# A hybrid transformer in fp32 on one core: the norm split into three steps among products, modulation rows in buffers of their own, one low part completed by an accumulating DMA, two whole pairs ahead of the blocked ones

## The chip, the cores and the metric

One NeuronCore of a Trainium2 chip runs the whole program in one launch. The metric is device time in microseconds (us), the median of several executions.

## The reference

Two layers work on 256 latent tokens and 256 context tokens of width 1024. Every branch is preceded by an RMS norm whose scale, shift and gate come from a modulation vector (`silu(c) @ mod_w`, nine vectors of 1024 for each layer and stream):

```python
lat = lat + 0.5 * mod[:, 0, 2] * _swiglu(_modulate(lat, norm_g[i, 0], mod[:, 0, 0], mod[:, 0, 1]), w13, w2)
...   # the same for the context tokens cx
h = _modulate(lat, norm_g[i, 1], mod[:, 1, 0], mod[:, 1, 1])
y = _short_conv_mixer(h, ...)                 # layer 0
y, _ = _gqa_mixer(h, hc, False, ...)          # layer 1: keys of both streams, queries of lat
lat = lat + mod[:, 1, 2] * y
lat = lat + 0.5 * mod[:, 2, 2] * _swiglu(_modulate(lat, norm_g[i, 2], ...), w13, w2)

def _swiglu(h, w13, w2):
    gte, up = jnp.split(h @ w13, 2, axis=-1)
    return (jax.nn.silu(gte) * up) @ w2       # hidden width 2816 = 22 x 128
```

In order there are: swiglu (0,0), the convolution mixer, swiglu (0,1), swiglu (1,0), attention, swiglu (1,1). The last one and the last projection are for the latent tokens alone.

## The kernel before

Everything is held with features on the 128 partitions and tokens along the free axis: `x` is 8 tiles of 128 features by 512 tokens. The first 256 columns (s = 0) are the latent tokens, the other 256 (s = 1) the context. The weights are fp32. Each is split into a rounded high part and a low part (`split`: ACT rounds, line 92; DVE subtracts, line 93), and each product is three matmuls, high·high, high·low and low·high (`mm3`, lines 116 to 118).

**Weights.** `load_raw` (line 86) brings 1 MB through SP's DMA queue into one of three buffers `wr`. `load_w` splits them into four halves `wh`/`wl`. The same three `wr` buffers also take the modulation rows.

**Modulation.** Each of the 236 units (`mod_unit`, line 136, tile `junk`) is one DVE instruction over 128 x 1024: a row block times the broadcast `silu(c)`, summed. Four units (two for a vector that one stream alone needs) share a 1 MB load. They are dealt out by `tick(n)`, which stands between products, and `mod_ready` makes those up that a consumer still lacks.

**A swiglu** goes in thirds of 8, 7 and 7 hidden tiles ("pairs": one gate tile and one up tile of `w13`), and after each third `project` multiplies by the matching part of `w2` and adds to `x` (`finish`, line 438). For 512 tokens a pair is either computed as it is (`w13_mm`, tiles `pg` and `pu`, 96 matmuls of 256 columns or 48 of 512) or as a `Pair`: a 2 x 2 blocked product with seven block products instead of eight (tiles `p` and `q`, 84 matmuls of 256 columns). For that DVE makes sums of weight blocks (`ws`, lines 548, 554, 556), and `Blocks.sums` makes sums of activation blocks (T1 to T4) once. The block A22 gets its own `w4h`/`w4l`. `head` uses A11 and A12 with the s = 0 activations, `five` to `four` the sums, and `four` of one pair comes after `six` of the next.

**The joint between two stages.** `tail_norm` is called as the last feature tiles of `x` are finished. `square_add` sums squares; `rms_inv` (line 226) adds them over partitions by four one-column matmuls (`ss`, line 231), takes the root on ACT and the reciprocal on DVE, and spreads the result by four matmul records (line 242). Then the normed activations are made (`t`, line 250, and `bh`/`bl` or `hh`/`hl`). Steps wait in the list `pending`, and `flush` runs them at chosen places. In the last project of a swiglu the last two feature tiles (m = 6, 7) are done for s = 0 first and then for s = 1, so that the norm of s = 0 runs beside the products of s = 1. The norm of s = 1 runs beside the s = 0 products of the next swiglu's pair 0 and the `head`s of pairs 1 and 2.

**Order.** A framework schedules the traced instructions: it keeps dependences, hands out buffers and chooses each engine's order when the program is built. Each engine then runs its own queue in order.

## Time and profile before

| | |
|---|---|
| three timed runs | 1613.83, 1616.15, 1619.61 us (median 1616.15) |
| the profiled execution | 1611.37 us, of which its span is 1609.5 |
| PE (matmuls) busy | 1576.1 us, 98% |
| DVE busy | 1332.4 us, 83% |
| ACT busy | 722.2 us, 45% |
| POOL | 0.2 us, 4 instructions |
| HBM read | 244.77 MB, 153 GB/s |

PE is the matrix engine, PEld its weight loads, DVE the vector engine, ACT the scalar engine, POOL the general one, SP the queue that issues nearly all DMAs. `PEclk` or "granted clock" is the share of full clock that the matrix engine was given. A matmul's recorded duration overlaps the next one's, so its cost is the distance from start to start. A line number in a profile is that of the kernel it was taken from.

### The profile page before, as it was taken

The numbers are of one execution on the slowest core, as the hardware profiler recorded it, in microseconds if no ns is written. First come the engines' busy times: TensorE is split into PE (matmuls) and PEld (weight loads), VectorE is DVE, ScalarE is ACT, GpSimd is POOL, SyncE is SP. The second block draws the span as 40 slices with busy tenths as digits, with TensorE's granted clock in tenths as the row PEclk, the third lists the DMA queues.
The fourth block names the chain that finished last, engine by engine and source line by source line (L and its number), as shares of the span: only waits on it lengthen the run. The fifth ranks groups of instructions, "written<-read, shape, count | busy, mean of one in ns | idle before, by whom it ended". The sixth has DMA issues, their size and how long they took to land.

```text
span 1609.5 us, 25613 instructions
## 1 busy us (share of the span) xinstructions
PE 1576.1 (98%) x10566; PEld 1450.1 (90%) x10566; DVE 1332.4 (83%) x2035; ACT 722.2 (45%) x1110; POOL 0.2 (0%) x4
## 2 busy tenths in 40 slices
PE   9999999999999999999999999999999999899999
PEld 6788998999888889899899889889899897789999
DVE  4988778879998889799797999898898789965554
ACT  5532452544322365335255465245254455454443
POOL 0000000000000000000000000000000000000000
PEclk9999999999999999999999999999999999999999
DMA  8456235234565513353433413452432463755453
GB/s 320 162 183 209 80 122 180 90 135 152 177 221 186 180 41 117 132 183 100 168 120 115 154 54 131 172 195 96 156 129 96 180 214 108 270 201 185 169 194 109
DMA packets 38277, 248.77 MB, mean 155 GB/s; under 512 B 5136, under 2 KB 6928, under 8 KB 12304
## 3 DMA queue, kind: packets, MB, share of 16 engines
q1 hardware_dynamic: 35712, 245.38, 43.7%
q10 hardware_dynamic: 2448, 1.76, 0.4%
q8 instruction: 82, 1.34, 0.3%
q14 instruction: 35, 0.29, 0.1%
HBM read 244.77 MB, written 1.05 MB: 153 GB/s over the span
## 4 chain that ended last, share of the span: by engine, by line
PE 82%; DVE 12%; DMA 3%; ACT 2%; issue 1%; DVEq 0%; ACTq 0%; SPq 0%
PE py L117 7%; PE py L116 7%; PE py L118 7%; PE p L116 6%; PE p L118 6%; PE p L117 6%; PE q L118 5%; PE q L116 5%; PE q L117 5%; DVE junk L136 4%; DVE wl L93 3%; PE pg L117 2%; PE pg L118 2%; PE pg L116 2%; PE pu L117 2%; PE pu L118 2%
## 5 line engine op out<-in xcount | busy, mean ns | idle before, releaser
L92 ACT ACTIVATE wh<-wr 128x1024 fp32r<-128x1024 f32 (+2 forms) x274 | 274.4, 1014 | 395.0 <-PE py L117 108.7
L93 DVE TENSOR_TENSOR wl<-wr,wh 128x1024 fp32r<-128x1024 f32 (+2 forms) x274 | 318.2, 1167 | 97.0 <-ACT wh L92 96.4
L136 DVE CUSTOM_DVE_ANT_0 junk<-wr,scbc,modb 128x1024 bf16<-128x1024 f32 x236 | 302.5, 1282 | 39.6 <-DMA wr<-in_modT 37.0
L117 PE MATMUL py<-gl,wh 128*128 128x512 f32 (+1 forms) x746 | 263.2, 353 | 0.0
L116 PE MATMUL py<-gh,wh 128*128 128x512 f32 (+1 forms) x746 | 263.1, 353 | 0.0
L118 PE MATMUL py<-gh,wl 128*128 128x512 f32 (+1 forms) x746 | 262.9, 352 | 0.0
L93 DVE TENSOR_TENSOR wl<-ws,wh 128x1024 fp32r<-128x1024 f32 x112 | 136.8, 1223 | 27.3 <-ACT wh L92 27.0
L118 PEld LDWEIGHTS py<-gh,wl 128*128 128x128 f32 x746 | 141.1, 189 | 19.1
L116 PEld LDWEIGHTS py<-gh,wh 128*128 128x128 f32 x746 | 141.2, 189 | 18.6
L117 PEld LDWEIGHTS py<-gl,wh 128*128 128x128 f32 x746 | 141.2, 189 | 18.0
L92 ACT ACTIVATE wh<-ws 128x1024 fp32r<-128x1024 f32 x112 | 117.8, 1057 | 76.4 <-PE p L117 34.2
L116 PE MATMUL p<-th,wh 128*128 128x256 f32 x448 | 126.8, 283 | 0.0
L117 PE MATMUL p<-tl,wh 128*128 128x256 f32 x448 | 126.8, 283 | 0.0
L118 PE MATMUL p<-th,wl 128*128 128x256 f32 x448 | 126.6, 283 | 0.0
L117 PE MATMUL q<-bl,wh 128*128 128x256 f32 x336 | 95.2, 283 | 0.0
L116 PE MATMUL q<-bh,wh 128*128 128x256 f32 x336 | 95.1, 283 | 0.0
L118 PE MATMUL q<-bh,wl 128*128 128x256 f32 x336 | 95.1, 283 | 0.0
L438 DVE SCALAR_TENSOR_TENSOR x<-py,G,x 128x256 f32<-128x256 f32 x168 | 74.2, 480 | 21.4 <-PE py L118 21.2
L116 PEld LDWEIGHTS p<-th,wh 128*128 128x128 f32 x448 | 86.0, 192 | 0.5 <-ACT sg L584 0.2
L117 PEld LDWEIGHTS p<-tl,wh 128*128 128x128 f32 x448 | 86.0, 192 | 0.3
L118 PEld LDWEIGHTS p<-th,wl 128*128 128x128 f32 x448 | 85.9, 192 | 0.0
L116 PE MATMUL pg<-hh,wh 128*128 128x256 f32 (+1 forms) x240 | 75.8, 316 | 4.6 <-ACT hh L260 4.6
(236 smaller groups left out, 4001.3 us busy)
## 6 DMA issues: line engine op xcount, KB each, us to landing
wr<-in_w SPq DMA_DIRECT2D x88, 1024.0 KB, 4.9
wr<-in_modT SPq DMA_DIRECT2D x67, 1024.0 KB, 4.9
wr<-in_w2b SPq DMA_DIRECT2D x32, 896.0 KB, 4.6
wr<-in_w2a SPq DMA_DIRECT2D x16, 1024.0 KB, 4.9
wr<-in_cw_cx SPq DMA_DIRECT2D x8, 1024.0 KB, 4.9
wr<-in_mod SPq DMA_DIRECT2D x5, 1024.0 KB, 7.4
wr<-in_cw_b SPq DMA_DIRECT2D x4, 1024.0 KB, 4.8
wr<-in_cw_out SPq DMA_DIRECT2D x4, 1024.0 KB, 4.9
```

The source lines that it names most:

```text
L92: nc.scalar.activation(out=hi, in_=src, func=AF.Copy)
L93: nc.vector.tensor_tensor(out=lo, in0=src, in1=hi.bitcast(F32), op=ALU.subtract)
L116: nc.tensor.matmul(ps, wh, mh, start=first, stop=False, **kw)
L117: nc.tensor.matmul(ps, wh, ml, start=False, stop=False, **kw)
L118: nc.tensor.matmul(ps, wl, mh, start=False, stop=last, **kw)
L136: nc.vector.tensor_tensor_reduce(out=junk, in0=raw[:, j * D : j * D + D], in1=scbc[:, v, :], scale=1.0, scalar=modb[:, l, col : col + 1], ...
L438: nc.vector.scalar_tensor_tensor(out=x[:, m, s * S : s * S + S], in0=ps[:, o : o + S], scalar=g[:, m, s : s + 1], in1=x[:, m, s * S : s * ...
```

## The change

1. `rms_inv` becomes `rms_sum` and `rms_all`. The norm of each stream now stands in `pending` as three steps (sums; spread and first half; second half), and `flush(1)` calls one at a time among products. The first matmul behind a step, and the norm's own matmuls, are held in program order.
2. The last project before a norm does its last three feature tiles (m = 5, 6, 7) by streams instead of its last two (`late` 3).
3. In swiglus (0,1) and (1,0) pairs 0 and 1 are computed as they are, ahead of the blocked ones, where only pair 0 was; the activation sums T1 to T4 and the weight sums are made in pieces between their products.
4. The low part of A22: ACT writes minus the high part, and a DMA issued by POOL adds the weights to it from HBM. DVE's subtraction (128 x 512) goes.
5. Modulation rows come by 512 KB into two buffers `mr` of their own; `wr` has two buffers instead of three. The first modulation vectors, which the matrix engine makes, are loaded by halves into the pool of activation tiles.
6. The calls of `tick` move within attention (none is left in the loop over heads), and the last projection's `ev` is 0.6 instead of 1.

```diff
-        raw = wp.tile([P, 2048], F32, name=nm("wr"), tag="wr", bufs=3)
+        raw = wp.tile([P, 2048], F32, name=nm("wr"), tag="wr", bufs=2)
...
+    pin = [False]
     def mm3(ps, w, m, first, last, more=False):
...
-        nc.tensor.matmul(ps, wh, mh, start=first, stop=False, **kw)
+        i = nc.tensor.matmul(ps, wh, mh, start=first, stop=False, **kw)
+        if pin[0]:
+            tc.keep_in_program_order(i)
+            pin[0] = False
...
+    def load_mod(l, ch, kt):
+        raw = mp.tile([P, D], F32, name=nm("mr"), tag="mr", bufs=2)
+        o = kt % 2 * D
+        nc.sync.dma_start(raw, a["modT"][l, ch * 4 + kt // 2, :, o : o + D])
+        return raw
...
-    def rms_inv(s, parts):
+    def held(ins):
+        return tc.keep_in_program_order(ins)
+    def rms_sum(s):
         pq = psmall("ss")
+        parts = accs[s], accs[s, "last"]
...
+        return pq, ri
+    def rms_all(pq, ri):
         for i in range(2):
-            nc.tensor.matmul(
+            held(nc.tensor.matmul(
...
     class Blocks:
-        def sums(self):
+        def sums(self, n):
...
-            tt(out=b11, in0=b12, in1=b11, op=ALU.subtract)
-            keep("T1", b11)
...
+            if n == 0:
+                tt(out=b11, in0=b12, in1=b11, op=ALU.subtract)
+                keep("T1", b11)
+            elif n == 1:
...
-    def flush(n=9):
+    def flush(n=99):
         while pending and n:
             pending.pop(0)()
+            pin[0] = True
             n -= 1
...
+                keep = []
+                def spread():
+                    keep.append(rms_all(*keep.pop()))
+                    rest(0, keep[0])
+                if s:
                     flush()
-                    pending.append(both_parts)
+                pending.extend(
+                    (lambda: keep.append(rms_sum(s)), spread, lambda: rest(1, keep[0]))
+                )
+                if (l, j) == (1, 2):
+                    flush()
...
-            wl = [get(m) for m in (6, 7)]
+            ms = range(KT - late, KT)
+            wl = [get(m) for m in ms]
...
             for s in range(2):
-                for i in range(2):
+                for i, m in enumerate(ms):
                     ps = psum("py")
-                    products(ps, wl[i], range(nk // 2), s * S, s * S + S)
-                    flush(1)
-                    products(ps, wl[i], range(nk // 2, nk), s * S, s * S + S)
-                    finish(6 + i, ps, s * S, s * S + S, gate, tail)
+                    products(ps, wl[i], range(cut), s * S, s * S + S)
+                    if i:
+                        flush(1)
+                    products(ps, wl[i], range(cut, nk), s * S, s * S + S)
+                    if i == 0:
+                        flush(1)
+                    finish(m, ps, s * S, s * S + S, gate, tail)
...
     class Pair:
...
-            split(*self.w["A22"], a22)
+            nc.scalar.activation(out=hi, in_=a22, func=AF.Copy)
+            nc.scalar.activation(out=lo, in_=hi.bitcast(F32), func=AF.Copy, scale=-1.0)
+            nc.gpsimd.dma_start(out=lo, in_=self.src[:, T2:1024], accum_op=ALU.add)
...
     def ffn(l, b, h, tot, gate, tail, gs=(), ev=1.5):
...
-                    w = load_w(a["w13"][l, b, 0])
-                    gs = [new_pair("g")]
-                    pp = psum("pg"), psum("pu")
-                    w13_mm(pp, w, h, range(KT), 0, S)
+                    w = [load_w(a["w13"][l, b, 0])]
+                    gs = [new_pair("g") for _ in range(2)]
+                    pp = [(psum("pg"), psum("pu")) for _ in range(2)]
+                    w13_mm(pp[0], w[0], h, range(4), 0, S)
+                    flush(1)
+                    w13_mm(pp[0], w[0], h, range(4, 6), 0, S)
+                    flush(1)
+                    w13_mm(pp[0], w[0], h, range(6, KT), 0, S)
+                    w.append(load_w(a["w13"][l, b, 1]))
+                    w13_mm(pp[1], w[1], h, range(KT), 0, S)
                     flush()
-                    for i in (1, 2):
-                        heads.append(Pair(a["w13"][l, b, i], h))
-                        heads[-1].head()
-                    w13_mm(pp, w, h, range(KT), S, T2)
-                    w13_post(pp, gs[0], 0, T2)
+                    h.sums(0)
+                    w13_mm(pp[0], w[0], h, range(KT), S, T2)
+                    w13_post(pp[0], gs[0], 0, T2)
+                    heads.append(Pair(a["w13"][l, b, 2], h))
+                    h.sums(1)
+                    heads[0].sums(0)
+                    w13_mm(pp[1], w[1], h, range(KT), S, T2)
+                    w13_post(pp[1], gs[1], 0, T2)
+                    heads[0].head()
+                    h.sums(2)
+                    heads[0].sums(1)
...
     def mod_pe(ch, q):
-        raw = load_raw(a["mod0"][ch, q])
+        raw = []
+        for i in range(2):
+            raw.append(hot("pm", F32))
+            nc.sync.dma_start(raw[i], a["mod0"][ch, q, :, i * 1024 : i * 1024 + 1024])
...
-                if n == 11:
-                    flush()
+                if n in (5, 11, 17):
+                    flush(1)
...
         if hd:
             mix(hd - 1, pts.pop(hd - 1))
-        tick(2)
...
-        by_pairs("wo"), lambda k, c0, c1: aos[k], KT, lazy_gate(1, 1), tail_norm(1, 2, hn), S, 0, 1,
+        by_pairs("wo"), lambda k, c0, c1: aos[k], KT, lazy_gate(1, 1), tail_norm(1, 2, hn), S, 0, 0.6,
```

## The prediction

> **What bounds the kernel now.** First the page's totals and its slices:
>
> ```profile
> span 1609.5 us, 25613 instructions
> PE 1576.1 (98%) x10566; PEld 1450.1 (90%) x10566; DVE 1332.4 (83%) x2035; ACT 722.2 (45%) x1110; POOL 0.2 (0%) x4
> ...
> DVE  4988778879998889799797999898898789965554
> ```
>
> PE is the bound, with DVE close behind it in many slices. PE's price per matmul comes from two full stretches of the view by windows (length, then busy time and count of PE, PEld, DVE, ACT, POOL; granted clock; DMA share and GB/s):
>
> ```profile
> 480.00:520.00 40.00, 40.00 (x178) 33.13 (x177) 34.25 (x52) 11.52 (x13) 0.00 (x0) 1.00 0.55 187
> ...
> 1440.00:1480.00 40.00, 40.00 (x336) 40.00 (x335) 23.63 (x31) 18.05 (x26) 0.00 (x0) 1.00 0.57 194
> ```
>
> 512 columns cost 40/178 = 0.2247 us, 256 columns 40/336 = 0.119. Next, the stretches where PE loses time. I count what is lost as length minus PE busy, plus (1 - clock) times length:
>
> ```profile
> 565.00:605.00 40.00, 36.46 (x276) 35.25 (x276) 34.13 (x50) 27.65 (x48) 0.00 (x0) 0.91 0.16 53
> 915.00:962.00 47.00, 42.64 (x317) 40.89 (x316) 42.89 (x64) 32.06 (x56) 0.00 (x0) 0.93 0.21 69
> 1055.00:1070.00 15.00, 13.42 (x88) 11.95 (x87) 14.96 (x21) 6.07 (x9) 0.00 (x0) 1.00 0.47 163
> ...
> 1333.00:1376.00 43.00, 35.18 (x224) 29.78 (x223) 43.00 (x108) 24.88 (x57) 0.00 (x0) 0.94 0.34 121
> 1376.00:1405.00 29.00, 26.88 (x210) 25.90 (x209) 26.84 (x46) 13.47 (x21) 0.00 (x0) 0.97 0.76 273
> 1405.00:1420.00 15.00, 10.28 (x62) 9.42 (x61) 14.91 (x30) 8.40 (x16) 0.00 (x0) 0.77 0.68 249
> ```
>
> Lost: 3.5 + 3.6 = 7.1 (joint into swiglu (0,1)); 4.4 + 3.3 = 7.7 (joint into (1,0)); 1.6; 7.8 + 2.6 = 10.4 (loop over heads); 2.1 + 0.9 = 3.0 (projection); 4.7 + 3.5 = 8.2 (joint into (1,1)). Together 38.0 us, nearly all that is to be had behind the start. The heads' 43.00 us are DVE's own bound. The same windows for the tile junk alone show modulation's share there (DVE busy, clock, DMA):
>
> ```profile
> 1333.00:1376.00 43.00, 12.48 (x10) 0.94 0.34 121
> ```
>
> PE's timeline names what ended the waits (start, length, instruction, idle time before it):
>
> ```profile
> 578.30 0.60 PE L242 MATMUL ss<-ident,ri 128*128 128x128 f32 x4
> 583.25 0.58 PE L116 MATMUL pg<-bh,wh 128*128 128x256 f32 x1 [3.03 <-ACT bh L92]
> ...
> 929.11 0.38 PE L231 MATMUL ss<-ones,sq 128*128 128x1 f32 x2 [1.22 <-ACT sq L214]
> ```
>
> From the spread of the context's norm to its first block lie 4.95 us, 5.65 plus to its low part (584.55). Last, DVE's distances from start to start, in its timeline: 1024 elements 1.14 us, 512 elements 0.60, a unit 1.20.
>
> ```profile
> 1059.33 1.22 DVE L93 TENSOR_TENSOR wl<-wr,wh 128x1024 fp32r<-128x1024 f32 x1
> 1060.47 0.87 DVE L438 SCALAR_TENSOR_TENSOR x<-py,G,x 128x256 f32<-128x256 f32 x2
> 1061.25 0.68 DVE L554 TENSOR_TENSOR ws<-wr,ws 128x512 f32<-128x512 f32 x1
> 1061.85 0.69 DVE L93 TENSOR_TENSOR w4l<-wr,w4h 128x512 fp32r<-128x512 f32 x1
> 1062.45 0.69 DVE L556 TENSOR_TENSOR ws<-wr,ws 128x512 f32<-128x512 f32 x1
> 1063.06 1.28 DVE L136 CUSTOM_DVE_ANT_0 junk<-wr,scbc,modb 128x1024 bf16<-128x1024 f32 x1
> 1064.26 0.09 DVE L136 DVE_READ_ACCUMULATOR2_ANT mod<- 128x1 f32 x1
> ```
>
> **PE's added work.** A whole pair is 96 matmuls of 256 columns, a blocked one 84: two pairs more as they are cost 24 x 0.119 = 2.9 us. `late` 3 splits one more feature tile in four projections: 3 x 21 + 24 = 87 matmuls of 512 become pairs of 256, 87 x (0.238 - 0.2247) = 1.2. PE is full there, so all of it counts: **+4.0**.
>
> **The joints into (0,1) and (1,0).** I read the built order of both kernels on each engine. Before, 11 products (1.3 us) stand between the context's spread and the first product that needs it. After, 54 do (6.5 us), against the 4.95 to 5.65 us above. DVE's queue between the reciprocal and the first block's low part now holds one weight split, one or two weight sums, seven `t`, one block sum and that low part: 1.14 + 0.60 + 7 x 0.40 + 1.14 + 1.14, and a unit in (0,1) alone, 1.20 = 8.0, beginning some 1 us ahead of the spread. The remaining stall lies between 0 and 1.5 us. The four sums matmuls no longer follow the last square directly, which ends the 1.22 above. I leave 2 us, clock included, in each joint: **-5.1 and -5.7**. Of the clock: in 915:962 no wait of PE exceeds 1.22 us, and 0.93 was granted all the same, so small stalls are charged for clock too.
>
> The Trainium skill, "TensorE: Matmul & The Clock Gate" (What's actually happening), has the clock halved after an idle window of about 3.4 us. By that rule stalls under it would cost no clock and each joint would give about 1 us more; 915:962 speaks against it.
>
> **Modulation moved ahead.** With buffers of their own the rows are no longer held behind weights. In DVE's built order all 236 units stand ahead of the last third of (0,1); before, 23 of them lay in 1333:1420. All their instructions move with them: 134 half loads on SP where 67 were, 0.33 us of issue each on SP, which waits mostly for buffers. Taken out of the late stages: at 1055 the 1.6 us go, **-1.6**. In the heads DVE's 43.0 less 12.5 is 30.5 us, below PE's own 43 - 10.4 = 32.6; I leave 3 us for the softmax chain, **-7.4**. In the projection 0.5 stays: **-2.5**. At the joint into (1,1) nothing covers the norm's chain, before or after; three units go ahead of it, and I leave 5 us: **-3.2**.
>
> What moves in must fit. From the first `seven` to the first residual update, the second third of (0,0) had 7 units among 55.0 us of DVE (counts by the distances above) and now has 21 among 70.7, for 66.2 us of PE. The last third has 70.5 likewise, and (0,1)'s first third 65.4 for 62.0. The surplus is 4.5 + 4.3 + 3.4 = 12.2 us. Behind the first of these the projection needs 35.1 of 42.5 us of DVE, and weights are split 3 to 5 us ahead, so most is absorbed: between 0 and 12.2, I take **+3**, nearer to 0 because 440:480 ran with DVE 39.61 of 40 busy and PE full.
>
> **A22's low part.** DVE loses 54 x 0.60 = 32 us, already in the sums above. ACT gains 54 x 0.63 = 34 us on 722, covered by its idle half. POOL waits for ACT's copy; only other such DMAs queue behind it, and PE's `four` waits for it two pairs (20 us) after its buffer comes free. The nearest landings are 3.8 us (rt, 64 KB) and 4.9 (1 MB): hidden, 0. If it took over 14 us, `four` would wait for the rest. **Two `wr` buffers:** a load holds one for 4.9 + 1.06 (ACT) + 2 x 1.14 = 8.2 us, so two feed a weight every 4.1 us, and (1,1), the fastest, uses one in 48 x 0.119 = 5.7: 0. SP's new waits on `mr` hold weight loads queued behind them; that is a rival below. **The start:** DMA is 89% busy in the first 40 us. Free loads can gain 4.4 us at most, rows ahead of weights lose as much: 0.
>
> Sum: 4.0 - 5.1 - 5.7 - 1.6 - 7.4 - 2.5 - 3.2 + 3 = -18.5. The profiled execution took 1611.37 us (its span and 1.9 around it), so 1592.9; the median of the runs is 4.8 above it, so **1598** as a median.
>
> **Rivals.**
> *DVE takes it back.* The whole surplus of 12.2 stays and the joints give half: -18.5 + 9.2 + 5.4 = -3.9, 1612. For it: DVE full in the pairs with 0 to 1 us of reserve. Against: 440:480.
> *Rows wait (slower).* DVE meets a unit whose row has not landed. The waits list has this:
>
> ```profile
> DVE junk L136 <- DMA wr<-in_modT: 37.0, 21, 4.8
> ```
>
> That is 1.76 us a time. In the thirds named and (0,1)'s second (16 units), 76 units now stand on 38 loads; a wait there delays splits, `four` and SP's next weight, with no reserve. Eleven such waits eat the gain; half of the 38 give -18.5 + 33.4, so 1631. Against: the units stand apart there, and a row has several us to land.
> *POOL holds DVE up (slower).* The trace has no POOL work. If each accumulating DMA held DVE by one 512-element instruction (0.69 us) in the 34 pairs of (0,0) and (0,1), that is 23.5: +5.0, 1621. From 0.54 us it decides.
>
> The Trainium skill, "SBUF — State Buffer" (Who interferes with whom), says that DVE and POOL lock each other out of a shared port for whole instructions, and that DMAs issued by POOL wait for their descriptors; no run here shows it yet.
>
> **How the numbers follow.** 0.3% (4.8 us) is about what a measurement can tell. My forecast has 0.68, its own range 1580 to 1609 (the low end: all 38.0 back and no surplus). DVE taking it back has 0.14: 0.06 faster, 0.07 same, 0.01 slower. Rows waiting 0.10, slower. POOL 0.08: 0.02 same, 0.06 slower. Faster 0.74, same 0.09, slower 0.17. With most of the second case inside, the range ends at 1616.
>
> **What would show it.** Windows around both joints should lose about 2 us each with a clock near 1, and no `junk` should stand in the heads, where PE is then the fuller engine. In 160:360 DVE should be over 95% busy with PE still full. PE idle there, released by `wl` behind `junk`, or `mr` loads leading DVE's waits, would prove me wrong; so would `w4l` products waiting for a DMA.

## The result: slower by 0.3%, and the profile after

| | before | after |
|---|---|---|
| median (16 runs each, timed together) | 1614.65 us | 1620.57 us |
| range | 1612.21 to 1619.61 | 1613.48 to 1625.37 |
| profiled execution | 1611.37 (span 1609.5) | 1624.71 (span 1622.9) |

The ratio is 1.0032, 95% interval 1.0019 to 1.0045: slower by 5 to 6 us. The forecast was 1598, with 1616 as the upper end.

The profiled execution of before lies 3.3 us under its median, that of after 4.1 over it. Of the 13.3 us between these two only 5.9 lie between the medians, so a difference of a few us in a single stage below may be of the execution and not of the kernel.

The page of the changed kernel has two lines that answer to those of before:

```profile
span 1622.9 us, 26150 instructions
...
DVE  4899999999899999989888579568577578755554
```

DVE is full for the first half and light afterwards, as forecast, since the units now stand there (the last at 850). The view by windows shows the same stretches as before, moved by what had been lost ahead of them (the columns are those of the prediction). The first two rows are those the prediction had no loss for, the start and the joint into the convolution:

```profile
0.00:40.00 40.00, 33.99 (x176) 22.62 (x177) 16.06 (x44) 20.41 (x37) 0.20 (x4) 0.87 0.80 300
390.00:425.00 35.00, 31.97 (x216) 30.45 (x215) 29.79 (x65) 15.21 (x30) 0.00 (x0) 0.85 0.39 136
577.00:617.00 40.00, 37.34 (x283) 36.76 (x282) 36.74 (x62) 23.65 (x43) 1.74 (x2) 0.91 0.41 121
937.00:984.00 47.00, 44.77 (x360) 44.39 (x359) 37.13 (x57) 31.37 (x54) 1.73 (x2) 0.96 0.33 98
1079.00:1094.00 15.00, 15.00 (x104) 13.95 (x103) 10.06 (x13) 5.43 (x8) 0.00 (x0) 1.00 0.22 71
1350.00:1391.00 41.00, 37.31 (x257) 32.66 (x256) 37.89 (x93) 27.90 (x60) 0.00 (x0) 1.00 0.24 83
1391.00:1418.00 27.00, 27.00 (x225) 26.75 (x226) 17.82 (x33) 14.06 (x25) 0.00 (x0) 1.00 0.23 79
1418.00:1434.00 16.00, 12.76 (x86) 12.30 (x85) 11.13 (x24) 8.20 (x16) 0.00 (x0) 0.79 0.38 132
...
280.00:320.00 40.00, 38.52 (x291) 36.99 (x291) 40.00 (x56) 20.68 (x32) 2.54 (x3) 1.00 0.61 177
```

and before:

```profile
0.00:40.00 40.00, 37.25 (x210) 24.41 (x211) 17.69 (x51) 21.61 (x45) 0.20 (x4) 1.00 0.89 320
380.00:420.00 40.00, 39.79 (x287) 37.28 (x287) 38.65 (x75) 17.70 (x34) 0.00 (x0) 1.00 0.39 135
```

The joint into (1,0) (the 937 row), the rest of (1,0) (1079), the heads (1350), the projection (1391) and the joint into (1,1) (1418) gained. The joint into (0,1) (577) hardly did, the start and the joint into the convolution (390) lost, and inside a pair stretch (280) PE now waits while DVE is busy 40.00 of 40.

To compare kernels stage by stage I take from each trace, for every two matmuls in a row, their distance from start to start less the full-speed distance (0.227 us for 512 columns, 0.120 for 256, 0.110 for one). The sum is what PE lost to waits and clock together, in us. A stage runs from one first `py` to the next, with its joint in it. Each column is one execution.

| PE lost in | before | after | steps only | DMA and `pm` out, start free |
|---|---|---|---|---|
| start, to the first `py` | 22.0 | 29.1 | 24.7 | 25.0 |
| other thirds of (0,0), (0,1) | 0.1 | 9.5 | 2.5 | 2.7 |
| end of (0,0), convolution | 1.9 | 9.7 | 4.7 | 3.2 |
| joint into (0,1), its first third | 7.8 | 9.6 | 3.0 | 6.6 |
| joint into (1,0), its first third | 9.8 | 4.6 | 2.8 | 4.8 |
| rest of (1,0) | 2.9 | 0.2 | 8.7 | 0.2 |
| attention | 15.5 | 11.6 | 26.5 | 13.2 |
| its projection, joint into (1,1) | 11.7 | 6.1 | 7.9 | 6.2 |
| sum | 71.7 | 80.4 | 80.8 | 61.9 |
| span less the sum | 1537.8 | 1542.5 | 1542.3 | 1542.3 |

The last row is PE's own work: 4.7 us more, where +4.0 was forecast. The third and fourth kernels are experiments (e9, which also has item 6 of the change, and e12), told below.

DVE's and PE's waits lists name what is new:

```profile
DVE junk L146 <- DMA mr<-in_modT: 35.9, 26, 2.8
...
PE ss L243 <- ACT sq L222: 6.3, 5, 1.7
PE q L118 <- ACT gm L602: 4.9, 4, 1.6
```

The second leads PE's list. Before, the same wait, of the norm's sums for a square, was

```profile
PE ss L231 <- ACT sq L214: 1.7, 2, 1.2
```

The DMA view of the changed kernel:

```profile
q1 hardware_dynamic: 46080, 245.39, 44.8%
q0 software_dynamic: 7776, 14.16, 5.3%
...
mr<-in_modT SPq DMA_DIRECT2D x134, 512.0 KB, 4.1
...
w4l<-in_w POOLq DMA_DIRECT2D x54, 256.0 KB, 5.1
```

Queue q0 carries the 54 accumulating DMAs. Per MB they held the 16 engines for 0.053 x 1622.9 / 14.16 = 6.1 us, the other loads (q1) for 0.448 x 1622.9 / 245.39 = 3.0 us.

### The profile page after: what moved, and what is told of

Read it like the earlier page. It is cut to its first block, busy times and chain, and to the rows that moved or that the text cites. A ratio compares the mean times of both kernels' runs of the same rounds, so it can differ in the third digit from the quotient of the medians.

```text
span 1622.9 us, 26150 instructions
## 1 busy us (share of the span) xinstructions
PE 1586.6 (98%) x10677; PEld 1461.5 (90%) x10677; DVE 1288.1 (79%) x1967; ACT 746.1 (46%) x1158; POOL 47.3 (3%) x58
## 3 DMA queue, kind: packets, MB, share of 16 engines
q1 hardware_dynamic: 46080, 245.39, 44.8%
q0 software_dynamic: 7776, 14.16, 5.3%
q10 hardware_dynamic: 2448, 1.76, 0.4%
## 4 chain that ended last, share of the span: by engine, by line
PE 63%; DVE 23%; DMA 7%; issue 4%; ACT 2%; DVEq 0%; ACTq 0%; SPq 0%
DVE junk L146 7%; DMA mr<-in_modT 6%; DVE wl L93 6%; PE py L118 5%; PE py L122 5%; PE py L123 5%; PE p L118 4%; PE p L123 4%; PE p L122 4%; PE q L118 3%; PE q L123 3%; PE q L122 3%; PE pg L122 3%; PE pg L123 2%; PE pg L118 2%
## 5 line engine op out<-in xcount | busy, mean ns | idle before, releaser
L146 DVE CUSTOM_DVE_ANT_0 junk<-mr,scbc,modb 128x1024 bf16<-128x1024 f32 x236 | 302.7, 1282 | 39.1 <-DMA mr<-in_modT 35.9
L122 PE MATMUL py<-gl,wh 128*128 128x512 f32 (+1 forms) x767 | 267.6, 349 | 1.5 <-DVE gl L93 1.5
L118 PE MATMUL py<-gh,wh 128*128 128x512 f32 (+1 forms) x767 | 268.1, 349 | 0.0
L122 PEld LDWEIGHTS py<-gl,wh 128*128 128x128 f32 x767 | 145.4, 190 | 19.2 <-DVE gl L93 1.9
L93 DVE TENSOR_TENSOR wl<-ws,wh 128x1024 fp32r<-128x1024 f32 x108 | 131.6, 1224 | 20.2 <-ACT wh L92 20.2
L118 PE MATMUL p<-th,wh 128*128 128x256 f32 x432 | 122.4, 283 | 0.1
L122 PE MATMUL p<-tl,wh 128*128 128x256 f32 x432 | 122.4, 283 | 0.0
L123 PE MATMUL q<-bh,wl 128*128 128x256 f32 x320 | 90.8, 284 | 0.0
L122 PE MATMUL q<-bl,wh 128*128 128x256 f32 x320 | 90.7, 283 | 0.0
L583 POOL DMA_DIRECT2D w4l<-in_w x54 | 47.1, 873 | 1207.2 <-ACT w4l L582 827.4
```

Of the source, the lines that this page charges most:

```text
L93: nc.vector.tensor_tensor(out=lo, in0=src, in1=hi.bitcast(F32), op=ALU.subtract)
L118: i = nc.tensor.matmul(ps, wh, mh, start=first, stop=False, **kw)
L122: nc.tensor.matmul(ps, wh, ml, start=False, stop=False, **kw)
L123: nc.tensor.matmul(ps, wl, mh, start=False, stop=last, **kw)
L146: nc.vector.tensor_tensor_reduce(out=junk, in0=raw, in1=scbc[:, v, :], scale=1.0, scalar=modb[:, l, col : col + 1], op0=ALU.mult, op1=ALU.add,
L583: nc.gpsimd.dma_start(out=lo, in_=self.src[:, T2:1024], accum_op=ALU.add)
```

## The experiments

Theories at the outset. **1**: units that run ahead fill DVE beyond its limit, so it comes late to the joints and in the thirds. **2**: the half loads of the first vectors delay the start. **3**: the accumulating DMAs, or POOL, hold DVE or the loads up. Below, a ratio is to the kernel before, timed alongside on the same chip; 0.1% is 1.6 us.

### Parts taken back one at a time

**e1_modold**: rows and first vectors as before.

```diff
-        raw = mp.tile([P, D], F32, name=nm("mr"), tag="mr", bufs=2)
-        nc.sync.dma_start(raw, a["modT"][l, ch * 4 + kt // 2, :, o : o + D])
+        raw = load_raw(a["modT"][l, ch * 4 + pair])     # wr, bufs=3
```

> The changed kernel with its modulation weights as before: rows of 1 MB through three shared wr buffers, first vectors by one load each. The other parts stay (norm in three held steps, late 3, two whole pairs, A22's low part by the accumulating DMA). The changed kernel lost, against before, 7 us up to the first py, about 11 us in the thirds of (0,0) and (0,1) and 8.6 us at the joint from (0,0) into the convolution, and won 10.4 us in attention's heads and projection. Theory 1 (rows with buffers of their own let every unit run early, where DVE is full, and PE waits for DVE there): the three losses go, most of the attention's gain goes too: 1620.6 - 7 - 11 - 8.6 + 8 = about 1602, with about 7 units per third of (0,0) and no DVE stretch of 40.00 of 40. Theory 3 (the accumulating DMAs or POOL hold DVE up): only the start comes back, the thirds and the joint stay: 1613 or, with the attention's gain lost, above 1620.

Measured 1627.74 us, ratio 1.0080 (1.0066 to 1.0095): slower still. The thirds and the joints improve (11 units instead of 32 in the stage of the second third of (0,0)), yet attention loses 26.4 us and the rest of (1,0) 10.0. Theory 1 has its effect and misses its size: with the rest of the change in place, keeping the units away from the late stages is worth more than they cost early. Much of attention's loss lies where item 6 of the change deals units out, as told at e9.

**e2_startold**: only the first vectors' loads as before.

```diff
-            raw.append(hot("pm", F32))
-            nc.sync.dma_start(raw[i], a["mod0"][ch, q, :, i * 1024 : i * 1024 + 1024])
+        raw = load_raw(a["mod0"][ch, q])
```

> The changed kernel with the first modulation vectors alone loaded whole through wr, as before, in place of two half loads in the hot pool; the later rows keep their own buffers. Theory 2 (the start's 7 us come from those half loads, which wait for buffers and split the transfers): the first py comes at 127 us in place of 134 and the time falls by 5 to 7, to 1614 or 1615. Rival (the start is late because the later rows' loads run freely beside the first weights): first py stays at 133 to 135, 1620.

Measured 1616.55, ratio 1.0017 (1.0005 to 1.0029). The first `py` comes at 130 us in place of 134. The interval overlaps the changed kernel's, so a gain of some 2 us is likely and not secured.

**e3_noacc**: A22's low part by ACT and DVE.

```diff
-            nc.scalar.activation(out=hi, in_=a22, func=AF.Copy)
-            nc.scalar.activation(out=lo, in_=hi.bitcast(F32), func=AF.Copy, scale=-1.0)
-            nc.gpsimd.dma_start(out=lo, in_=self.src[:, T2:1024], accum_op=ALU.add)
+            split(hi, lo, a22)
```

> The changed kernel with A22's low part by ACT and DVE as before, and no accumulating DMA; the rest stays. Theory 1: DVE has 54 x 0.6 = 32 us more to do, 24 of it in the thirds where it is already full, so PE loses more there: 1620.6 + 8 to 24 = 1629 to 1645. Theory 3 (the accumulating DMAs hold DVE or the load queues up, by over 0.6 us each): the time falls below 1620, by 54 x 0.27 = 15 us if each holds DVE for POOL's 0.87 us, to 1606.

Measured 1605.66, ratio 0.9953 (0.9934 to 0.9971). This is the largest finding: DVE gets 54 instructions back and the kernel is 0.79% (13 us) faster than with the DMA. DVE's surplus, the trouble I had foreseen, cannot be by itself what stalled PE in the second third of (0,0), since DVE is as full here and PE loses nothing there: the recorded durations of DVE's instructions, which overlap a little, sum to 1.09 of that stage, and to 1.07 in the changed kernel. (The profile of e3 is of its slowest run, 1613.53; below, e7 stands for the kernels without the DMA.)

**e4_hold**: units pinned to their place in program order.

```diff
+        held(unit)      # the tensor_tensor_reduce of mod_unit
```

> The changed kernel with every modulation unit held in program order on DVE, so that a row in its own buffer no longer lets units run ahead of their place; loads, buffers and all else stay. In its order 20 units fall in the projection into attention, 9 in attention's own projection, 7 in (1,1), and the thirds of (0,0) hold fewer. Theory 1: the 11 us of the thirds and 8 us of the joint into the convolution go, the start's 7 stay, 2 to 6 us of the attention's gain go: 1620.6 - 19 + 4 = about 1606. Theory 3, or the transfers themselves (the loads come no later than in the changed kernel): thirds unchanged, 1620 or above.

Measured 1686.53, ratio 1.0444 (1.0429 to 1.0458). A pinned unit stands behind whatever was traced before it on DVE, so 236 pins fix most of the queue. PE's waits list is led by the norms:

```profile
PE pg L118 <- ACT hh L277: 16.8, 5, 11.3
```

This tells nothing about theory 1: it measures the pin.

### What in the low part's DMA costs

**e5_noacc_start**: the diffs of e2 and e3 together.

> Two parts of the change undone together: A22's low part by ACT and DVE, and the first modulation vectors by one load each through wr. Undone alone, the first gave 15 us against the changed kernel (1605.7), the second 4 us (1616.5). If the two prices lie in different places (start, and thirds with the joint into the convolution) they add: 1620.6 - 15 - 4 = 1601.6, with first py at 130 us. If both act through the same thing (how full DVE is made with units ahead of the convolution), the sum is less: 1605 or above.

Measured 1604.89, ratio 0.9953 (0.9938 to 0.9968): as e3. Without the DMA the half loads cost nothing that can be told.

**e6_negdve**: ACT's second copy moved to DVE, the DMA kept.

```diff
-            nc.scalar.activation(out=lo, in_=hi.bitcast(F32), func=AF.Copy, scale=-1.0)
+            nc.vector.tensor_scalar(out=lo, in0=hi.bitcast(F32), scalar1=-1.0, ..., op0=ALU.mult)
```

> The changed kernel, with ACT's second copy (w4l = -w4h) done by DVE; the accumulating DMA stays. ACT then has what it had before, POOL and the transfers are as in the changed kernel. Theory ACT (ACT's in-order queue, 54 x 0.63 us longer, brings gm, sg and wh late to PE): about 1606, as without the DMA. Theory DMA (POOL's issue and 14 MB more of transfers bring rows and weights late): 1618 to 1621. Theory units (with the splits off DVE the planner puts 21 units in a third in place of 18, and those wait for rows): 19 and 18 units stand in the first two pair stretches here, so about 1608.

**e7_actextra**: the copy kept, the DMA out.

```diff
-            nc.gpsimd.dma_start(out=lo, in_=self.src[:, T2:1024], accum_op=ALU.add)
+            nc.vector.tensor_tensor(out=lo, in0=a22, in1=hi.bitcast(F32), op=ALU.subtract)
```

> The changed kernel with ACT's second copy kept, but DVE then writing the low part over it, with no DMA from POOL: ACT is loaded as in the changed kernel, DVE as before it. Theory ACT: about 1618 to 1621, or more, since DVE's split now waits for that copy too. Theory DMA: about 1606. Theory units (18 units in each of those stretches, as without the copy): about 1606.

Measured 1621.40 (1.0042, 1.0028 to 1.0057) with the DMA and 1603.49 (0.9943, 0.9930 to 0.9956) without. ACT's copy is free, the DMA is not. In e6's worst place, DVE's timeline shows how (start, length, instruction, idle time before it and who ended it):

```profile
827.25 1.21 DVE L93 TENSOR_TENSOR wl<-ws,wh 128x1024 fp32r<-128x1024 f32 x1
832.54 1.28 DVE L146 CUSTOM_DVE_ANT_0 junk<-mr,scbc,modb 128x1024 bf16<-128x1024 f32 x1 [4.08 <-DMA mr<-in_modT]
```

then ACT's and PE's:

```profile
838.82 1.06 ACT L92 ACTIVATE wh<-ws 128x1024 fp32r<-128x1024 f32 x1 [9.21 <-DVE ws L571]
839.78 0.35 ACT L604 COPY gm<-q 128x256 f32<-128x256 f32 x1
```

```profile
840.18 0.58 PE L118 MATMUL q<-bh,wh 128*128 128x256 f32 x1 [6.68 <-ACT gm L604]
```

That unit's row, issued at 822.24, is the only `mr` load of its microsecond, so the view of the tile there gives its landing:

```profile
DMA to landing us min/median/max: 10.2/10.2/10.2
```

Two accumulating DMAs (issued at 821.0 and 826.0) and one weight load (9.0 us to landing) are in flight with it. DVE stands still 4.08 us in the middle of a queue with no slack, the weight sum behind it is late, ACT waits for that sum ahead of the copy `gm`, and PE waits 6.68. In e7, beside the same pair stretch, the rows land after 3.5 to 6.4 us and DVE's waits for them there are 0.79 and 0.68 us.

Over (0,0) to (1,0), all loads grouped by what is in flight with them (1 us or more of overlap with another load, 0.5 us with a POOL DMA), median us from issue to landing:

| | e7, no DMA | after | e6 | e17 |
|---|---|---|---|---|
| `wr` (w13), alone | 4.79 | 4.78 | 4.77 | 4.87 |
| `wr`, beside a POOL DMA | | 5.07 | 5.02 | 5.70 |
| `wr`, beside a load | 5.00 | 5.07 | 4.91 | 4.92 |
| `wr`, beside both | | 5.97 | 5.92 | 6.62 |
| `mr`, alone | 3.68 | 3.70 | 3.69 | 3.71 |
| `mr`, beside a load | 4.56 | 4.47 | 4.12 | 4.51 |
| `mr`, beside both | | 5.80 | 6.34 | 5.05 |

The loads keep their times except where they meet a POOL DMA: where three are in flight, a weight or a row lands 0.5 to 2.2 us later than where two are, and at worst a row takes 10.2.

**e13_spare_acc, e14_spare_plain, e15_spare_act**: the order of e3, and DMAs into a tile that nobody reads.

```diff
+            split(hi, lo, a22)
+            sp = mp.tile([P, 448], F32, name=nm("spare"), tag="spare", bufs=1)
+            nc.scalar.activation(out=sp, in_=hi[:, :448].bitcast(F32), func=AF.Copy, scale=-1.0)
+            nc.gpsimd.dma_start(out=sp, in_=self.src[:, T2 : T2 + 448], accum_op=ALU.add)
```

e14 leaves out `accum_op`; e15 also issues the DMA by `nc.scalar`.

> The changed kernel with A22's low part by ACT and DVE, as in the kernel that gave 1605.7, and beside it DMAs that nobody reads: per pair ACT copies -w4h into a spare tile (448 of 512 columns) and POOL's accumulating DMA adds A22 there. DVE's and PE's order, and what waits for what, are as without; only the DMAs and the copy are more (the copy alone cost nothing: 1603.5). Theory transfers (the DMAs delay the loads beside them, and DVE meets rows too early): 1612 to 1618, and loads beside such a DMA as late as in the changed kernel (wr 6.0, mr 5.8 us). Theory order (the price lies in where the planner puts units and weight steps once DVE no longer has the low part, not in the DMA): 1603 to 1607.

> The same with a plain DMA from POOL's queue into the spare tile. If the adding makes the price: 1603 to 1607 here while the adding one gives 1612 or more. If it is the bytes or POOL's queue: the same time as the adding one.

> The same plain DMA issued by ACT, on the queue that its other DMAs use, in place of POOL's. If POOL's queue (its packets, or its issue of 0.5 to 0.9 us) makes the price: 1603 to 1607, and rows beside it no later than without. If the bytes alone do: as the plain one from POOL.

Measured 1616.70 (1.0014, 1.0005 to 1.0022), 1611.53 (0.9986, 0.9973 to 0.9999) and 1611.58 (0.9985, 0.9974 to 0.9995). For a plain DMA POOL's queue is not the price: ACT's gives the same. But ACT's waits list of e13 shows a flaw, a wait for the one spare tile that holds ACT's splits:

```profile
ACT spare L583 <- DMA spare<-in_w: 9.7, 5, 3.2
```

**e17_spare2_acc, e18_spare2_plain**: two spare tiles of 384 columns, adding and plain.

```diff
-            sp = mp.tile([P, 448], F32, name=nm("spare"), tag="spare", bufs=1)
+            sp = mp.tile([P, 384], F32, name=nm("spare"), tag="spare", bufs=2)
```

> The kernel with adding DMAs that nobody reads, with two spare tiles of 384 columns in place of one of 448. With one tile ACT waited for the landing of the DMA before it, 9.7 us in 5 waits, which held its weight splits; with two it need not. Theory transfers: three quarters of the changed kernel's bytes, so 8 to 11 us above 1604.5 (the mean of 1605.7 and 1603.5, the same order without DMAs), 1612 to 1616. If ACT's waits made the time of the one-tile kernel: 1604 to 1607, and the price in the changed kernel lies in the planner's order after all.

> The same with plain DMAs, two spare tiles. One tile gave 1611.5, with 6.6 us of ACT's waits in it. If the bytes alone delay the loads: 1608 to 1612. If only the adding does, or ACT's waits did: 1603 to 1606.

Measured 1612.09 (0.9980, 0.9968 to 0.9992) and 1608.20 (0.9963, 0.9949 to 0.9977), and ACT no longer waits for the tile. Without a DMA the same kernel gave 0.9953 (e3, the same order of instructions) and 0.9943 (e7). Against these the adding DMAs cost 0.27 to 0.37%, 4 to 6 us, for three quarters of the bytes with nobody waiting for them; the interval overlaps that of e3 by a little and that of e7 not at all. The plain ones cost 0.10 to 0.20%, 2 to 3 us, which their interval does not tell from nothing. Adding costs more than copying: the intervals of e13 and e14 do not overlap, though ACT's wait for the one tile is in both, and those of e17 and e18 do by a little.

The stages agree. By the measure of the table PE loses under 0.1 us in the second and third thirds of (0,0) in e3, e5, e7, e9, e10, e12 and e16, which have no such DMA, and in e1, which has the adding one but no rows in buffers of their own. It loses 2.8 us there in the changed kernel, and 0.6 to 4.8 in e2, e6, e13, e14, e15, e17 and e18, which have one beside such rows. (e8 loses 2.1 without a DMA; its DVE waits far more for rows, as told below.) So **the transfers themselves cost time**, and the loads beside them, late by the table above, are the likely way.

Scaled to all the bytes the spare DMAs give 4 to 6 x 4/3 = 5 to 8 us. The real one costs 13 against e3, 10 between e2 and e5, and 16 between e6 and e7, where DVE has one instruction for the low part on both sides. The 2 to 11 us that remain are open. DVE's other order alone does not explain them: the stages of the second and third thirds of (0,0) have 32 and 30 units in the changed kernel, 30 and 28 in e6 and 29 and 27 in e7, yet e6 is as slow as the changed kernel.

**e11_plain**: the real low part with a plain DMA and DVE's subtraction behind it.

```diff
-            nc.gpsimd.dma_start(out=lo, in_=self.src[:, T2:1024], accum_op=ALU.add)
+            nc.gpsimd.dma_start(out=lo, in_=self.src[:, T2:1024])
+            nc.vector.tensor_tensor(out=lo, in0=lo.bitcast(F32), in1=hi.bitcast(F32), op=ALU.subtract)
```

> As the kernel with ACT's second copy kept and DVE making the low part (1603.5), and POOL's DMA back but as a plain one: it writes A22 itself into w4l after ACT's copy, and DVE then takes the high part off it in place. Same bytes, same engine that issues, same moment; only the adding is gone. If the adding is what delays the loads beside it: 1603 to 1607, loads beside such a DMA no longer than others (wr 5.0, mr 4.5 us). If it is the 14 MB more or POOL's queue: 1614 to 1621, loads as late as in the changed kernel (wr 6.0, mr 5.8 us beside it), more if DVE waits for the landing itself.

Measured 1659.49, ratio 1.0289. It answers another question: DVE itself now waits for landings,

```profile
DVE w4l L584 <- DMA w4l<-in_w: 64.5, 40, 4.0
```

and PE loses 115.5 us by the measure of the table, 59.8 in e7: 64.5 us of waiting in DVE's queue, and what the DMA does beside, came out as 56 us. In these stages most of DVE's lateness turns into time; how much of the 56 is the DMA's own price, no run tells.

### Steps and rows

**e9_steps_only**: before, with the held steps, `late` 3 and two whole pairs: the diffs of e1, e2 and e3 together. Item 6 of the change (the moved calls of `tick`, `ev` 0.6) stays in it.

> The kernel before with the norm in three held steps, late 3 and the two whole pairs alone: modulation weights by 1 MB through three wr buffers, first vectors through wr, A22's low part by ACT and DVE. Against it stands the same kernel with the accumulating DMA (1627.7). Theory DMA-by-rows (the accumulating DMAs cost because they delay the rows that DVE, filled with units, meets too early): without own rows DVE has reserve, so the DMA costs little here, and this kernel gives 1623 to 1628. Rival (the DMA costs by itself, wherever it is): 1612, 16 us below. Either way the distance to 1604.9 is what rows with buffers of their own are worth beside the steps.

**e10_rows_only**: before, with rows in buffers of their own and nothing else.

```diff
-        raw = wp.tile([P, 2048], F32, name=nm("wr"), tag="wr", bufs=3)
+        raw = wp.tile([P, 2048], F32, name=nm("wr"), tag="wr", bufs=2)
...
+    def load_mod(l, ch, kt):
+        raw = mp.tile([P, D], F32, name=nm("mr"), tag="mr", bufs=2)
```

> The kernel before with rows of 512 KB in two mr buffers and two wr buffers alone: norm in one piece, late 2, blocks in all pairs, no accumulating DMA, first vectors through wr. If steps and rows add, and the steps alone are worth what the joints showed (3 us at the one into (0,1), 5 at the one into (1,0), less 4.3 of added products and some 4 at the start), the rows' share is all of the gain: about 1605 to 1608. If the steps need the rows (DVE otherwise has units of its own in the attention and joints) or the rows need the steps, it stays at 1611 to 1614.

Measured 1624.85 (1.0068, 1.0055 to 1.0080) and 1612.00 (0.9985, 0.9976 to 0.9995). Neither kernel does much good: the parts together (e5) give 0.9953. Without rows of their own the steps gain in both joints about what I had forecast (7.8 to 3.0 and 9.8 to 2.8 in the table), but attention loses 26.5 us in place of 15.5, the rest of (1,0) 8.7 in place of 2.9. DVE's windows of `junk` alone in e9, in (1,0) and in the heads, where the changed kernel has none:

```profile
1058.00:1073.00 15.00, 7.24 (x6) 0.77 0.45 157
1346.00:1393.00 47.00, 6.18 (x5) 0.97 0.32 112
```

The heads are not where attention loses more: PE loses 7.3 + 1.4 = 8.7 us in that window, before 10.4 with 10 units. Some 10 of the 11 us lie ahead of them. The joint into attention has a part in that (the changed kernel, with no unit in attention, loses 2 us more there than before). The rest stands where item 6 put the calls of `tick` that had been in the loop over heads. There e9 has 13 units, and PE's window is:

```profile
1290.00:1346.00 56.00, 48.60 (x321) 45.52 (x322) 47.94 (x84) 25.20 (x43) 0.00 (x0) 0.92 0.62 212
```

Before, from 1283 to 1333, 7 units stand, and PE is busy 49.62 of 50 us at clock 1.00. So e9's 0.7% is not the price of the steps alone: the moved calls are in it, and no run has the steps without them.

With the rows alone the opposite happens. The joint into (0,1) gets units it did not have, and its stage loses 17.8 us (before 7.8): the joint's window, and the same for `junk` alone (no unit stood there before, nor in the same joint of e9):

```profile
565.00:605.00 40.00, 33.81 (x230) 32.72 (x228) 36.73 (x57) 23.57 (x41) 0.00 (x0) 0.83 0.25 87
...
565.00:605.00 40.00, 7.68 (x6) 0.83 0.25 87
```

This pair answers e9's question as well: the DMA costs 1627.74 against 1624.85 (0.12%, intervals overlapping) where rows share `wr`, and 1616.55 against 1604.89 (0.64%, 10 us) where they run ahead. By these two pairs the DMA's price needs the rows that run ahead and the full DVE they make.

**e8_mr1**: e5 with one `mr` buffer.

```diff
-        raw = mp.tile([P, D], F32, name=nm("mr"), tag="mr", bufs=2)
+        raw = mp.tile([P, D], F32, name=nm("mr"), tag="mr", bufs=1)
```

> As the kernel with the two parts undone (A22's low part by DVE, first vectors through wr), with one mr buffer in place of two. A load then waits until the unit before it is read, so units run ahead less: 13 in the pair stretches of (0,0) where there were 17 or 18, 29 in the convolution's stretch where there were 50, and 11 in those of (1,0) where there were none. Theory 1 (DVE filled over its limit ahead of the convolution is what stalls PE in the thirds and at the joints into the convolution and (0,1)): some 6 of the 12 us lost there come back, 2 are lost in attention: 1596 to 1599. Rival (with one buffer DVE waits for most rows, about 4 us from issue to landing less the work in between): DVE's waits for rows at least double, 1610 to 1625.

Measured 1614.97, ratio 1.0008 (0.9993 to 1.0022): the rival. Units stand spread out, and DVE waits for many more rows (24.4 us, 21 times, in e3):

```profile
DVE junk L146 <- DMA mr<-in_modT: 99.1, 61, 3.8
```

**e12_start_free, e16_late2**: e5 with the very first norm not held; the same with `late` 2.

```diff
-        return tc.keep_in_program_order(ins)
+        return ins if free[0] else tc.keep_in_program_order(ins)   # free[0] until the first norm is made
...
-                gate, tail if end else None, tot, 3 if end and tot == T2 else 0, ev, between,
+                gate, tail if end else None, tot, 2 if end and tot == T2 else 0, ev, between,   # e16 alone
```

> The kernel with both parts undone (A22's DMA and the first vectors' half loads, 1604.9), and the sums and spreads of the very first norm no longer held in program order on PE; those behind it stay held. In traces of kernels with the held start PE loses 25 to 29 us up to the first py, before 22.0, part of it in spreads that stand ahead of products for the first vectors. If that hold is the cause: 2 to 4 us less, 1601 to 1603, first py at 127 or 128 us. If not: 1605.

> The kernel with both parts undone and the first norm free (1604.6), with late 2 in place of 3. Its nominal PE time falls by 29 matmuls' worth per projection, 1.2 us in all by the prediction's price; with 24 matmuls fewer between a spread and the projection's end the held steps have less cover. If late 3 pays: 2 to 5 us slower, lost at the joints, 1606 to 1610. If only the two pairs and the steps do: 1603 to 1605.

Measured 1604.63 (0.9944, 0.9932 to 0.9957) and 1605.62 (0.9941, 0.9929 to 0.9953). Neither can be told from e5: the hold at the start costs and `late` 3 gains nothing measurable. e3, e5, e7, e12 and e16 all beat the kernel before by 0.5 to 0.6%, and the changed one by 0.8 to 0.9%; what they share is the change without its accumulating DMA.

## Why the prediction was wrong

**The step that failed first is the term "A22's low part": 0.** I asked whether the DMA's own reader would wait. It does not: the waits lists have no `w4l` product and no DVE instruction behind it. I did not ask what 14 MB more do to the 512 KB rows and 1 MB weights in flight beside them, in stages where I had myself put DVE at its limit. In its place the runs show 10 to 16 us, 4 to 6 of them with DMAs that nobody waits for and that have three quarters of the bytes. With that term right, the forecast would have been 1608 to 1614; the joint into (0,1), the start and the joint into the convolution make up most of the rest.

**"Rows wait" was the rival that came nearest**, by another cause. I gave it 1.76 us a wait and a break-even at 11 waits. The page has 26 waits of 1.4 us, 35.9 in all, and before 37.0 in 21: the sum did not grow. What grew is what a wait costs. Before, DVE had reserve in the pair stretches (7 units); now it has none, and PE pays. The argument against it ("a row has several us to land") took the landing as fixed at its median, while a load that meets others took up to 8.5 us in the changed kernel and 10.2 in e6. In e13 and e17 DVE's waits for rows are 4 to 5 us more than in e7, and ACT's for weights 2 to 7 us more (44.7 in e7, 46.3 and 51.3). How much of either reaches PE is not shown wait by wait.

**"POOL holds DVE up"** fell. DVE's 512-element `ws` takes 0.689 us both beside POOL's instruction (33 of them) and away from it (69), and for plain DMAs a queue other than POOL's gave the same time. That this rival's 1621 is the time measured is chance: these DVE instructions were not held. By the Trainium skill, "SBUF — State Buffer" (Who interferes with whom), a DVE instruction with two SBUF inputs contends only with a GpSimd one that reads SBUF, and these rows show none with POOL issuing DMAs. The Trainium skill, "DMA: Bandwidth & Descriptors" (Queues, rings and completion order), has each DMA engine take turns between its queues packet by packet. The late loads beside POOL's DMAs agree with that; how the packets alternate, no run here shows.

**The joint into (0,1), -5.1:** the mechanism is shown by e9, with the steps and no rows in buffers of their own (-4.8). In the changed kernel the stage gained nothing (+1.8), as units stand in the joint: 8 between 577 and 617, none before. Rows in buffers of their own bring them there, since e1, which lacks only these and the half loads, loses 3.1 us in that stage. I counted units between the reciprocal and the first block's low part, and there stands none; five stand ahead of the reciprocal (576.8 to 584.7), between the last residual updates, and delay the squares. I read "all units ahead of the last third" without asking what they do in the joints on the way.

**The sums behind the last square** failed with it. The prediction has the four sums matmuls no longer follow the last square directly, which was to end a wait of 1.22 us. In the changed kernel this wait leads PE's list: 6.3 us in five joints, 1.7 of them in the one into (0,1) and 1.4 in the one into (1,0), against 1.7 in two before. In each of the five the granted clock is one half for 3.4 or 6.8 us, from 0.2 to 2.8 us after the wait's end. The rows alone (e10), where nothing is held, have 4.5 us of this wait in three, the steps without rows (e9) 2.1 in three, so it goes more with the rows that run ahead than with the hold. Three readings were off as well, with little effect: from 578.30 to 584.55 are 6.25 us and not 5.65, still under the 6.5 of the 54 products; 21 units and not 23 lie between 1333 and 1420; and the median of the 16 runs is 3.3 us above the profiled execution and not 4.8.

**The joint into the convolution** was not in the sum at all, since nearly nothing was lost there before (1.9). It lost 7.8 us more. The number of units does not explain that: 21 stand between 350 and 425, and before 22. By the measure of the table the rows alone (e10) lose about 1 us in this stage, the steps without them (e9) 4.7, the kernels with both and no DMA 2.5 to 6.1, and e2, e6, e13 and e17, with an adding DMA, 4.0 to 4.3. So some 3 us go with the steps; the rest is in this execution and not explained.

**The start, 0 (at most 4.4 either way):** +7.1 in that profile, +2.7 to +6.4 in the kernels without the DMA. By the prediction's measure most of it is clock: 0.87 over the first 40 us, before 1.00. DMA's busy share there fell from 0.89 to 0.80, so the loads were held, not short of bandwidth. What holds them stays open. The executions with the half loads lose 24 to 29 us up to the first `py` and those of the kernels with the new steps and whole loads 24 to 29 as well, so the 4 us by which e2's first `py` comes earlier may be scatter, and the held first norm costs nothing measurable (e12). Before and e10, with the norm in one piece, lose 22.0 and about 24.

**Right:** PE's added work (+4.7, forecast +4.0); the joint into (1,0) (-5.2 in the table, forecast -5.7); the rest of (1,0) (-2.7, -1.6); the heads, by their window 41.0 - 37.3 = 3.7 us left with clock 1.00, forecast 3. The attention stage shows only -3.9, as the joint into it, for which no term stood in the sum, lost more than before (3.9 us from 1291 to 1321, before 0.5 from 1270 to 1300). The projection and the joint into (1,1) gave -5.6 in the table and -4.6 by their windows, forecast -5.7: more than forecast in the first, half in the second. **DVE's surplus, +3:** without the DMA the other thirds lose about 1 to 6 us, so the term was of the right size; with it they lose 9.5 in the changed kernel.

## What to carry to other kernels

Price a transfer that nobody waits for by the loads that will be in flight beside it, and by how much reserve the engine has that waits for those. Two edits that both move the same work cannot be summed from a profile of neither: here the kernel without rows of their own was 0.7% slower, the one with these rows alone 0.15% faster, and the one with everything but the DMA and the half loads 0.5% faster. An experiment that is named after one part must leave out all others: e9 kept item 6, and most of attention's added loss in it stands where that item puts units. Where buffers are set free, count where the freed work lands in each joint of the built order, those that lose nothing today among them.

## What the hardware showed beside that

Waits of a fraction of a microsecond can cost clock. In the joint into the convolution PE was busy 2.43 of 3.40 us, with four waits of 0.17 us and the first 0.30 of one of 0.63 in it, and the granted clock then fell to one half for the next 6.8 us. The view by windows:

```profile
406.70:410.10 3.40, 2.43 (x12) 1.55 (x11) 3.40 (x8) 1.75 (x4) 0.00 (x0) 1.00 0.00 0
...
410.10:416.90 6.80, 6.47 (x30) 6.47 (x31) 4.15 (x8) 0.26 (x1) 0.00 (x0) 0.50 0.42 157
```

At a wait of 6.68 us in e6, which ended at 840.18, it was low for 6.8 us as well (838.6 to 845.4). So the length of one wait does not give its price in clock. Nor does their sum: from 280 to 320 PE waited 1.5 us and from 1350 to 1391 3.7 us, and both had 1.00. What decides, these runs do not settle. The Trainium skill, "TensorE: Matmul & The Clock Gate" (What's actually happening), has the half clock after an idle window of about 3.4 us; the length of these stretches agrees with such windows, but the window ahead of the half clock was not idle here: PE was busy for 2.43 us of it.
